# A modulation buffer of its own, loaded and applied by halves, and later modulation steps spread over four stages

## The chip, the cores and the metric

The kernel runs on one core of one Trainium2 chip. The metric is the device time of one execution in microseconds (us); lower is better. The engines that matter here are TensorE (PE, matrix products), VectorE (DVE), ScalarE (ACT), GpSimd (POOL) and the queues through which SyncE (SP), ACT and POOL issue their DMA transfers. Each engine runs its own list of instructions in a fixed order.

## The reference

The first of two transformer blocks is the one that the change touches; the second block behind it and the final norm are unchanged. Cut to what matters:

```
sh1, sc1, g1, sh2, sc2, g2 = split(silu(c) @ w_mod + b_mod, 6)          # latent rows; w_mod is 1024 x 6144
csh1, csc1, ...            = split(silu(c_ctx) @ w_mod + b_mod, 6)      # context rows
h_lat = rms_norm(x, norm_mix_g) * (1 + sc1) + sh1                       # 256 tokens x 1024
h_ctx = rms_norm(ctx, norm_mix_g) * (1 + csc1) + csh1                   # 256 tokens x 1024
p_lat, p_ctx = h_lat @ w_in, h_ctx @ w_in                               # 1024 x 9280: q, k, v, gates, ...
y_lat = token_mixer(...)      # gated delta rule (8 heads, chunks of 64, a triangular solve per chunk)
                              # + gated linear attention (4 heads), merged through gates
x = x + g1 * y_lat
h = rms_norm(x, norm_ffn_g) * (1 + sc2) + sh2
x = x + g2 * moe_ffn(h)       # top 4 of 32 experts, w_gu 32 x 1024 x 2048, w_down 32 x 1024 x 1024
```

Only `sh1, sc1, csh1, csc1` (columns 0 to 2047 of `w_mod`) are needed before the mixer. The columns 2048 to 6143 (`g1, sh2, sc2, g2`) are needed after it.

## The kernel before

**Head.** `pre` loads x and ctx over SP's queue, normalises them (ACT squares, DVE scales), and transposes the 512 tokens by 1024 features on PE into `xT` (L202, ACT copies L203). The modulation of the mixer is group 0 of `mod_steps`: eight steps k, and in each two tiles `w` of 128x1024 (512 KB) come over SP's queue (L161) into a ring of six buffers that all weight tiles share. Four matmuls a step (L162) add the product of the two conditioning vectors with the tile into one PSUM tile "mod". Behind the last step DVE adds the bias (L172), PE transposes (L178), DVE copies the result into `modT` (L180) and forms `sc1` (L209), DVE (L211) and ACT (L213) apply scale and shift to `xT`, and `split` makes the pair `hh` (high part, ACT, L49) and `hl` (low part, DVE, L50). Products in full precision are three matmuls of high and low parts (`mm3`, L76 to L78).

**Gates' weights and projections.** `gates` loads 64 columns of `w_in` into one more ring tile by two DMAs on ACT's queue (L259, L260: runs of 32 floats, 128 bytes), splits it into `whi`/`wlo` and makes the gates. `gdn_pair` works on two of the eight heads of the delta rule: six tiles of `w_in` (128x8x128, runs of 512 bytes) over POOL's queue (L399), q, k and v projections, a convolution on DVE (L372), and blocks of the triangular matrices that go through DRAM: stores `blkD` (L496) and loads `X` (L501), both on SP's queue. `L505` on DVE begins the triangular inverse of a pair: 31 pairs of DVE instructions (L515, L516), each of which needs the one before it. Its result goes out and back through SP's queue (L521 to L529), and PE's levels (L556 and on) and the scan follow. The four pairs overlap: the projections of pair n+1 stand ahead of the levels of pair n.

**Fill.** Behind each pair stand tasks that don't depend on the inverse, listed in `gdn`: `lat[0]` to `lat[15]` (`lat_act`: a projection of the latent rows, 48 matmuls, for the merge), and the 16 steps of `mod_steps(1)` and `mod_steps(2)`, whose tiles come over SP's queue (L161) into the same ring. Before:

```
fill = [lat[0:1] + m1[0:3] + lat[1:2] + m1[3:6] + lat[2:3] + m1[6:8],
        lat[3:4] + m2[0:3] + lat[4:5] + m2[3:6] + lat[5:6] + m2[6:8],
        lat[6:10], lat[10:] + [...]]
```

**What sets the order.** A scheduler puts each engine's instructions into one list when the program is built, from the order in which the code is written and from when buffers come free. On the chip each engine, and each DMA queue's issue, follows its list in order and waits where the next instruction's inputs or buffers aren't ready. Behind the mixer the 32 experts' weights are streamed (L1308, L1330), then block 2 follows.

Of the kernel before, what the change touches and what calls it, by code (L numbers as in the profile page):

```python
# [7 lines left out]
F32 = mybir.dt.float32  # L8
# [88 lines left out]
def pre(K, dbg=None):  # L97
# [8 lines left out]
    def G(shape=None):  # L106
        return psum.tile([P, 512], F32, name="g", bufs=2)
# [25 lines left out]
    nc.sync.dma_start(xc, I["ctx"].rearrange("o (t p) d -> p (o t) d", p=P))  # L133

# [14 lines left out]
    def mod_steps(g):  # L149


        hold = {}

        def step(k):
# [14 lines left out]
            for r in range(2 if g == 0 else 1):
                nc.gpsimd.dma_start(brow[r:P:32, :], bm)  # L170
            row = brow
            nc.vector.tensor_add(row, ps, brow)  # L172
            if g:
                nc.gpsimd.dma_start(K.modD[g - 1].rearrange("(q n) -> q n", n=512), row[0:P:32, :])
                return
            pt = G()
            for b in range(4):
                nc.tensor.transpose(pt[:, b * P:(b + 1) * P], row[:, b * P:(b + 1) * P], K.ident)  # L178
            for r in range(2):
                nc.vector.tensor_copy(K.modT[:, r].rearrange("p h (q b) -> p (h q) b", b=4),  # L180
                                      pt.rearrange("p (b q r) -> p r q b", b=4, r=32)[:, r])
# [17 lines left out]
    for k in range(8):  # L199
        p = G()  # L200
# [7 lines left out]
    for r in range(2):
        nc.vector.scalar_tensor_tensor(K.sc1[:, r], K.modT[:, r, 1], 1.0, K.nmg, op0=OP.add, op1=OP.mult)  # L209
    for k in range(8):  # L210
        nc.vector.tensor_scalar(xT[:, k, 0:256], xT[:, k, 0:256], K.sc1[:, 0, k:k + 1], K.modT[:, 0, 0, k:k + 1],  # L211
                                op0=OP.mult, op1=OP.add)
        nc.scalar.activation(xT[:, k, 256:512], xT[:, k, 256:512], AF.Identity, scale=K.sc1[:, 1, k:k + 1],  # L213
                             bias=K.modT[:, 1, 0, k:k + 1])
        split(K, xT[:, k, :], hh[:, k, :], hl[:, k, :])
# [15 lines left out]
def gates(K, dbg=None):  # L231
# [159 lines left out]
def gdn_pair(K, pr):  # L391
# [258 lines left out]
def gdn(K, dbg=None):  # L650
# [4 lines left out]
    m1, m2 = K.mod_steps(1), K.mod_steps(2)  # L655
    fill = [lat[0:1] + m1[0:3] + lat[1:2] + m1[3:6] + lat[2:3] + m1[6:8],
            lat[3:4] + m2[0:3] + lat[4:5] + m2[3:6] + lat[5:6] + m2[6:8],
            lat[6:10], lat[10:] + [lambda: gla_gates(K, 0), lambda: gla_proj(K, 0), lambda: gla_gates(K, 1)]]
# [1353 lines left out]
```

## Time and profile before

| | us |
|---|---|
| median of 3 runs | 2082.15 |
| fastest and slowest of them | 2078.74, 2091.74 |
| the profiled execution | 2083.65 |
| its span in the trace | 2081.9 |
| PE busy in the span | 1898.8 (91%) |
| DVE busy | 965.6 (46%) |
| ACT busy | 652.5 (31%) |

The mean granted TensorE clock was 0.954 of full speed. Times in the trace count from the start of the span. The head ends near 64 us, the four pairs of the delta rule reach to about 520 us, and from about 800 to 1700 us the experts' weights are streamed. Busy shares are means over stages that have different limits; what counts for a change in the first 500 us is who waits for whom there.

### The profile page before, as it was taken

How to read it: one execution, taken by the hardware profiler on the slowest of the kernel's cores; microseconds unless marked ns; L12 is line 12 of the kernel's file. 1: busy time of each engine (PE TensorE's matmuls, PEld its weight loads, DVE VectorE, ACT ScalarE, POOL GpSimd, SP SyncE). 2: the span in 40 equal slices, each digit the busy share in tenths (PEclk: the TensorE clock that was granted, in tenths of full speed). 3: DMA queues.
4: the chain of work that ended last, by engine and by line, in shares of the span. 5: the costliest groups of instructions: out<-in, count | busy, mean ns of one | idle time of the engine just before them, and what ended most of it. 6: DMA issues, size and time to landing. Idle time of an engine off the chain costs nothing. (4 is left out here: it accounts for less than half of the span.)

```text
span 2081.9 us, 27700 instructions
## 1 busy us (share of the span) xinstructions
PE 1898.8 (91%) x10742; PEld 1159.6 (56%) x10743; DVE 965.6 (46%) x2245; ACT 652.5 (31%) x1369; POOL 184.0 (9%) x247
## 2 busy tenths in 40 slices
PE   4796989799998999999999999999999889989998
PEld 1664768687986763333333333333333228779997
DVE  2797785857464641212122221221211137676777
ACT  2553545467554420000000000000000004555554
POOL 1343122211112000000000000000000000000000
PEclk8798999899999989999999999999999988998999
DMA  7347654437544689999999999999999994433551
GB/s 261 77 122 206 183 169 116 112 103 206 169 151 151 254 325 417 417 414 418 417 416 418 418 416 417 418 416 417 418 418 416 417 345 139 140 102 121 183 182 41
DMA packets 191939, 569.60 MB, mean 274 GB/s; under 512 B 47919, under 2 KB 90776, under 8 KB 158650
## 3 DMA queue, kind: packets, MB, share of 16 engines
q1 hardware_dynamic: 160064, 507.19, 63.1%
q0 software_dynamic: 13392, 47.72, 7.4%
q10 hardware_dynamic: 18346, 12.86, 2.5%
q8 instruction: 86, 1.41, 0.3%
q14 instruction: 51, 0.42, 0.1%
HBM read 555.22 MB, written 12.50 MB: 273 GB/s over the span
## 5 line engine op out<-in xcount | busy, mean ns | idle before, releaser
L50 DVE TENSOR_TENSOR wlo<-w,whi 128x1024 fp32r<-128x1024 f32 (+1 forms) x185 | 223.9, 1211 | 132.6 <-ACT whi L49 129.8
L1308 PE MATMUL pg<-w,xT 128*64 128x512 f32 x1024 | 274.4, 605 | 3.5 <-DMA w<-in_w_gu_dram 3.4
L1308 PE MATMUL pl<-w,xT 128*64 128x512 f32 x1024 | 268.1, 593 | 0.0
L49 ACT ACTIVATE whi<-w 128x1024 fp32r<-128x1024 f32 (+1 forms) x189 | 197.3, 1047 | 217.8 <-PE pj L77 70.4
L1330 PE MATMUL po<-w,aT 128*64 128x512 f32 x1024 | 239.9, 608 | 7.1 <-DMA w<-in_w_down_dram 5.7
L1230 ACT ACTIVATE th<-ga 128x512 f32<-128x512 f32 x32 | 20.2, 632 | 613.8 <-DVE ga L1228 613.8
L1338 DVE TENSOR_TENSOR o<-po,g 64x512 f32<-64x512 f32 x64 | 44.1, 689 | 260.1 <-PE po L1330 259.4
L1308 PEld LDWEIGHTS pl<-w,xT 128*64 128x64 f32 x1024 | 75.2, 137 | 146.4 <-issue 146.4
L1330 PEld LDWEIGHTS po<-w,aT 128*64 128x64 f32 x1024 | 69.5, 139 | 141.7 <-issue 121.9
L1308 PEld LDWEIGHTS pg<-w,xT 128*64 128x64 f32 x1024 | 65.2, 136 | 139.4 <-issue 115.9
L1228 DVE TENSOR_SCALAR ga<-pg 128x512 f32<-128x512 f32 x32 | 22.1, 691 | 244.8 <-PE pg L1308 244.8
L77 PE MATMUL pj<-wlo,hh 128*128 128x256 f32 x384 | 116.2, 303 | 2.8 <-DVE wlo L50 2.8
L76 PE MATMUL pj<-whi,hh 128*128 128x256 f32 x384 | 115.2, 300 | 2.9 <-ACT whi L49 2.9
L78 PE MATMUL pj<-whi,hl 128*128 128x256 f32 x384 | 114.6, 299 | 0.0
L76 PE MATMUL pj<-hh,whi 128*128 128x512 f32 (+1 forms) x264 | 100.9, 384 | 12.6 <-ACT hh L49 9.1
L372 DVE SCALAR_TENSOR_TENSOR acc<-padl,taps,acc 128x256 f32<-128x256 f32 x192 | 104.3, 557 | 10.1 <-ACT acc L365 8.0
L78 PE MATMUL pj<-hh,wlo 128*128 128x512 f32 (+1 forms) x264 | 100.0, 380 | 5.9 <-DVE wlo L50 5.7
L77 PE MATMUL pj<-hl,whi 128*128 128x512 f32 (+1 forms) x264 | 100.9, 382 | 0.1
L1288 POOL CAST se<-sel 128x128 fp32r<-128x128 f32 x32 | 22.4, 702 | 828.4 <-PE pl L1292 828.4
L1267 PEld LDWEIGHTS tr<-S,h 128*128 128x128 f32 x480 | 57.9, 191 | 48.6 <-issue 34.9
L77 PEld LDWEIGHTS pj<-wlo,hh 128*128 128x128 f32 x384 | 78.0, 203 | 11.0 <-DVE wlo L50 4.2
L1360 PE MATMUL y<-o,PwT 128*128 128x512 f32 (+1 forms) x136 | 72.2, 641 | 13.0 <-DVE o L1338 10.2
(682 smaller groups left out, 3601.7 us busy)
## 6 DMA issues: line engine op xcount, KB each, us to landing
w<-in_w_gu_dram SPq DMA_DIRECT2D x256, 1024.0 KB, 18.2
w<-in_w_down_dram SPq DMA_DIRECT2D x139, 1024.0 KB, 20.0
w<-in_w_in_dram POOLq DMA_DIRECT2D x72, 512.0 KB, 5.4
w<-in_w_mod_dram SPq DMA_DIRECT2D x48, 512.0 KB, 6.9
w<-in_w_up_dram SPq DMA_DIRECT2D x22, 1024.0 KB, 5.1
w<-in_w_in_dram SPq DMA_DIRECT2D x8, 1024.0 KB, 9.8
gbc<-gD ACTq DMA_DIRECT2D x16, 256.0 KB, 6.2
actD<-la ACTq DMA_DIRECT2D x16, 256.0 KB, 5.0
```

The lines of the kernel that those rows point to most:

```text
L49: K.nc.scalar.activation(hi, src, AF.Copy)
L50: (lo_eng or K.nc.vector).tensor_sub(lo, src, hi)
L76: nc.tensor.matmul(out, ah, bh, start=first, stop=False, **kw)
L77: nc.tensor.matmul(out, ah, bl, start=False, stop=False, **kw)
L78: nc.tensor.matmul(out, al, bh, start=False, stop=last, **kw)
L372: eng.scalar_tensor_tensor(al, pl[:, dy:dy + 4, dx:dx + 64], w, al, op0=OP.mult, op1=OP.add)
L1267: nc.tensor.matmul(p[:, kk * P:kk * P + m * CAP], h2[:, t, k * P:(k + 1) * P], S[:, t, e0:e1].rearrange("p e c -> p (e c)"), start=(kk == ...
L1288: nc.gpsimd.tensor_copy(se, sel[:, e, :, None].to_broadcast([P, 2, CAP]))
L1308: nc.tensor.matmul(pp[hs, :], xT[:, k, :], w[:, off + half * 512:off + half * 512 + 512], start=False, stop=(k == 7), skip_group_check=True)
L1330: nc.tensor.matmul(po[dh * CAP:(dh + 1) * CAP, :], aT[:, k % 4, (k // 4) * CAP:(k // 4 + 1) * CAP], w[:, kk * 1024 + dh * 512:kk * 1024 + ...
L1338: nc.vector.tensor_mul(outs[e // 2][e % 2 * CAP:(e % 2 + 1) * CAP, dh * 512:(dh + 1) * 512], po[hs], K.g2[hs])
L1360: nc.tensor.matmul(ps[dh], PwT[g][hs, t, :], outs[g][hs, dh * 512:(dh + 1) * 512], start=(g > 0), stop=True)
```

## The change

The head's modulation no longer goes through the ring. A buffer `wm` of its own holds all of group 0, loaded by 16 DMAs of 128x2x512 (512 KB each, runs of 2 KB); the first eight hold shift and scale for features 0 to 511, the second eight those for 512 to 1023. Between the halves comes the first `w_in` tile `w0`, behind them the gates' weights `wg`, and then the other five tiles of pair 0, all on SP's queue (before: ACT's and POOL's). The modulation is computed, transposed and applied one half after the other. In the fill, one modulation step stands behind each `lat` task, and the steps reach over three stages; the first three stages have four `lat` tasks each (before three, three and four).

```
+    w3 = I["w_in"].rearrange("o (k p) n -> p (o k) n", p=P)
+    K.wg = ring.tile([P, 8, P], F32, name="w")
+    nc.gpsimd.memset(K.wg[:, :, 64:], 0.0)
+    K.w0 = ring.tile([P, 8, P], F32, name="w")
+    wm = early.tile([P, 2, 8, 2, 512], F32, name="wm")
+    for b in range(2):
+        for k in range(8):
+            nc.sync.dma_start(wm[:, b, k], I["w_mod"][0, k * P:(k + 1) * P, 0:2048]
+                              .rearrange("p (s b n) -> p s b n", s=2, b=2)[:, :, b])
+        if b == 0:
+            nc.sync.dma_start(K.w0, w3[:, :, 0:P])
+        else:
+            nc.sync.dma_start(K.wg[:, :, 0:32], w3[:, :, 4096:4128])
+            nc.sync.dma_start(K.wg[:, :, 32:64], w3[:, :, 7200:7232])
...
-    for f in mod_steps(0):
-        f()
...
+    for b in range(2):
+        ps = psum.tile([P, 512], F32, name=("mod", "po")[b], bufs=1)
+        for k in range(8):
+            for s in range(2):
+                nc.tensor.matmul(ps[32 * s:32 * s + 32, :], csP[:, k, :], wm[:, b, k, s], start=(k == 0), stop=(k == 7),
+                                 skip_group_check=True)
+        nc.vector.tensor_add(rows[b], ps[:64], rows[b])
+        pt = G()
+        for i in range(4):
+            nc.tensor.transpose(pt[:, i * 64:(i + 1) * 64], rows[b][:, i * P:(i + 1) * P], K.ident[:64, :64])
...
+        for k in range(b * 4, b * 4 + 4):
+            nc.vector.tensor_scalar(xT[:, k, 0:256], xT[:, k, 0:256], K.sc1[:, 0, k:k + 1], K.modT[:, 0, 0, k:k + 1],
+                                    op0=OP.mult, op1=OP.add)
...
-    nc.scalar.dma_start(wg[:, :, 0:32], w3[:, :, 4096:4128])
-    nc.scalar.dma_start(wg[:, :, 32:64], w3[:, :, 7200:7232])
-    wgh, wgl = wsplit(K, wg, P)
+    wgh, wgl = wsplit(K, K.wg, P)
...
-    ws = []
-    for i in range(6):
+    ws = [] if pr else [K.w0]
+    for i in range(len(ws), 6):
         w = K.ring.tile([P, 8, P], F32, name="w")
         col = i % 3 * 1024 + pr * 256 + i // 3 * P
-        nc.gpsimd.dma_start(w, w3[:, :, col:col + P])
+        (nc.gpsimd if pr else nc.sync).dma_start(w, w3[:, :, col:col + P])
...
+    m = K.mod_steps(1) + K.mod_steps(2)
+    fill = [[f for i in range(4) for f in (lat[pr * 4 + i], m[pr * 5 + i])] + m[pr * 5 + 4:(pr + 1) * 5 + pr // 2]
+            for pr in range(3)]
+    fill.append(lat[12:] + [lambda: gla_gates(K, 0), lambda: gla_proj(K, 0), lambda: gla_gates(K, 1)])
```

Behind the edit at `pre` the line numbers are higher by 16 to 18: L161, L162, L172 of `mod_steps` become L176, L177, L187, the transposes of group 0 L227, `blkD` L513, `X` L518, L505 becomes L522, and L515/L516 become L532/L533.

**Place 1, SP's queue at the start of the program.** `w` are ring tiles, `gD` and `blkD` are DRAM tiles of the gates and of pair 0. Before:

```order
L132 DMA xlat<-in_x_dram 128x2x1024
L133 DMA xctx<-in_ctx_dram 128x2x1024
L161 DMA w<-in_w_mod_dram 128x1024 x16
L326 DMA gD<-grow 64x128
L161 DMA w<-in_w_mod_dram 128x1024 x4
```

SP's queue after:

```order
L132 DMA xlat<-in_x_dram 128x2x1024
L133 DMA xctx<-in_ctx_dram 128x2x1024
L142 DMA wm<-in_w_mod_dram 128x2x512 x8
L146 DMA w<-in_w_in_dram 128x8x128
L142 DMA wm<-in_w_mod_dram 128x2x512 x8
L148 DMA w<-in_w_in_dram 128x8x32
L149 DMA w<-in_w_in_dram 128x8x32
L416 DMA w<-in_w_in_dram 128x8x128 x5
L343 DMA gD<-grow 64x128
L176 DMA w<-in_w_mod_dram 128x1024 x2
```

The gates' weights and pair 0's tiles have moved onto this queue, behind the modulation's 16 transfers.

**Place 1, DVE at the end of the head.** `la` is the row of modulation values with its bias, `sc` is `sc1`. Before:

```order
L172 TENSOR_TENSOR la<-mod,la 128x512
L50 TENSOR_TENSOR wlo<-w,whi 128x1024
L180 COPY modT<-g 128x16 x2
L209 SCALAR_TENSOR_TENSOR sc_303<-modT,vecs 128x8
L50 TENSOR_TENSOR wlo<-w,whi 128x1024
L209 SCALAR_TENSOR_TENSOR sc_303<-modT,vecs 128x8
L211 TENSOR_SCALAR xT<-xT,sc_303,modT 128x256 x6
L50 TENSOR_TENSOR hl<-xT,hh 128x512 x2
L211 TENSOR_SCALAR xT<-xT,sc_303,modT 128x256 x2
L50 TENSOR_TENSOR hl<-xT,hh 128x512 x6
```

DVE there after:

```order
L224 TENSOR_TENSOR la<-mod,la 64x512
L230 COPY modT<-g 128x2x4 x2
L231 SCALAR_TENSOR_TENSOR sc_249<-modT,vecs 128x4 x2
L233 TENSOR_SCALAR xT<-xT,sc_249,modT 128x256 x4
L50 TENSOR_TENSOR hl<-xT,hh 128x512 x4
L224 TENSOR_TENSOR la<-po,la 64x512
L230 COPY modT<-g 128x2x4 x2
L231 SCALAR_TENSOR_TENSOR sc_249<-modT,vecs 128x4 x2
L233 TENSOR_SCALAR xT<-xT,sc_249,modT 128x256 x4
L50 TENSOR_TENSOR wlo<-w,whi 128x1024 x2
L50 TENSOR_TENSOR hl<-xT,hh 128x512 x4
```

The split of the gates' weights (`wlo`) stood between the bias and `modT`; it now stands behind both halves of the modulation, ahead of the last four `hl`.

**Place 2, PE at the first fill.** `pj_1391` is a projection of pair 1, `pj_1989` the one of `lat[0]`, `g_1436` a transpose of pair 1's keys, `w_2052` and on the modulation's tiles. Before:

```order
L78 MATMUL pj_1391<-hh_117,wlo_1388 128x512
L162 MATMUL mod_2051<-w_2060,csP_105 32x512
L162 MATMUL mod_2051<-w_2064,csP_105 32x512 x2
L162 MATMUL mod_2051<-w_2068,csP_105 32x512 x2
L162 MATMUL mod_2051<-w_2072,csP_105 32x512 x2
L162 MATMUL mod_2051<-w_2144,csP_105 32x512
L424 MATMUL g_1436<-ident_62,kT_1292 128x128 x4
L76 MATMUL pj_1989<-whi_1990,hh_117 128x256
```

PE there after (rows of `lat[0]` stand between `pj_1391` and the first of these):

```order
L78 MATMUL pj_1989<-whi_1990,hl_141 128x256
L76 MATMUL pj_1989<-whi_2018,hh_140 128x256
L177 MATMUL mod_2051<-w_2128,csP_128 32x512 x2
L177 MATMUL mod_2051<-w_2132,csP_128 32x512 x2
L76 MATMUL pj_2066<-whi_2067,hh_140 128x256
L441 MATMUL g_1436<-ident_62,kT_1292 128x128 x4
L177 MATMUL mod_2051<-w_2204,csP_128 32x512 x2
L77 MATMUL pj_1989<-wlo_2019,hh_140 128x256
```

The run of modulation matmuls behind `pj_1391` is gone; the first half of `lat[0]` stands in its place, and `g_1436` stands behind that.

**Place 2, DVE at the start of pair 0's inverse.** `acc` are the convolutions of pair 1, `L` and `X` the inverse of pair 0. Before:

```order
L372 SCALAR_TENSOR_TENSOR acc_1416<-padl1_346,taps_353,acc_1416 128x256
L459 TENSOR_TENSOR dk_1289<-d_1274,kds_464 128x8
L505 SCALAR_TENSOR_TENSOR L_991<-X_988,isd_470,L_991 128x1024
L372 SCALAR_TENSOR_TENSOR acc_1416<-padl1_346,taps_353,acc_1416 128x256
L507 MEMSET X_988 128x512
L378 SCALAR_TENSOR_TENSOR kT_1292<-th_1384,acc_1367 128x512
```

DVE there after:

```order
L476 TENSOR_TENSOR dk_1289<-d_1274,kds_466 128x8
L50 TENSOR_TENSOR wlo_1991<-w_1985,whi_1990 128x1024
L522 SCALAR_TENSOR_TENSOR L_991<-X_988,isd_472,L_991 128x1024
L524 MEMSET X_988 128x512
L389 SCALAR_TENSOR_TENSOR acc_1367<-padl0_348,taps_359,acc_1367 128x256
L526 MEMSET X_988 64x16 x2
L389 SCALAR_TENSOR_TENSOR acc_1367<-padl0_348,taps_359,acc_1367 128x256
L532 TENSOR_TENSOR xtmp_997<-L_991,X_988 128x31
```

The inverse begins ahead of twelve convolution taps that stood in front of it, and a split of `lat[0]`'s weights stands ahead of it.

**Place 3, SP's queue from pair 2's stores to pair 3's loads.** The rows between them that carry the inverse's result are left out. Before:

```order
L496 DMA blkD_2269<-mt 32x16x32 x4
L501 DMA X<-blkD_2269 64x1024 x2
...
L496 DMA blkD_3449<-mt 32x16x32 x4
L501 DMA X<-blkD_3449 64x1024 x2
```

SP's queue there after:

```order
L513 DMA blkD_2308<-mt 32x16x32 x4
L176 DMA w<-in_w_mod_dram 128x1024 x2
L518 DMA X<-blkD_2308 64x1024 x2
L176 DMA w<-in_w_mod_dram 128x1024 x4
...
L176 DMA w<-in_w_mod_dram 128x1024 x4
L513 DMA blkD_3532<-mt 32x16x32 x4
L176 DMA w<-in_w_mod_dram 128x1024 x2
L518 DMA X<-blkD_3532 64x1024 x2
L176 DMA w<-in_w_mod_dram 128x1024 x4
```

Sixteen loads of modulation tiles, each of which needs a free ring buffer, now stand among the transfers of pairs 2 and 3.

## Rows read from the trace of the kernel before

**Rows 1.** The page, section 4: the chain that ended last, by engine.

```profile
PE 16%; DVE 2%; ACT 1%; issue 0%; DMA 0%; DVEq 0%; ACTq 0%
```

**Rows 2.** DMA view, first 60 us: GB/s in 40 slices of 1.5 us.

```profile
GB/s 0 117 412 299 333 293 254 89 350 421 412 418 325 385 306 347 161 150 380 243 238 336 402 378 339 194 267 282 287 290 222 36 0 0 194 232 265 8 5 74
```

**Rows 3.** Waits in the first 60 us, SP's queue and PE: total, times, longest.

```profile
SPq L161 <- PE mod L162: 12.3, 5, 4.2
...
PE mod L162 <- DMA w<-in_w_mod_dram: 8.8, 5, 3.7
```

**Rows 4.** Timeline of the head: start, length, instruction, idle time before it.

```profile
6.56 23.70 SPq L161 DMA_DIRECT2D w<-in_w_mod_dram  x16
...
26.84 0.66 PE L202 MATMUL g<-ident,xn 128*128 128x128 f32 x4
...
30.66 1.10 ACTq L260 DMA_DIRECT2D w<-in_w_in_dram  x1
...
47.00 2.00 ACT L49 ACTIVATE whi<-w 128x1024 fp32r<-128x1024 f32 x2 [18.87 <-DMA w<-in_w_in_dram]
...
49.23 0.25 DVE L180 COPY modT<-g 128x16 f32<-128x16 f32 x2
...
51.90 1.14 ACT L49 ACTIVATE hh<-xT 128x512 fp32r<-128x512 f32 x2
...
52.57 1.01 PE L76 MATMUL pj<-hh,whi 128*128 128x512 f32 x2 [9.09 <-ACT hh L49]
...
64.63 0.38 PE L76 MATMUL pj<-hh,whi 128*128 128x256 f32 x1
```

**Rows 5.** Windows of the head: length, busy us of PE, PEld, DVE, ACT, POOL; PEclk, DMA share, GB/s.

```profile
12.00:20.00 8.00, 7.29 (x22) 1.49 (x22) 5.48 (x33) 1.23 (x3) 0.00 (x0) 1.00 0.99 387
...
40.00:46.00 6.00, 2.59 (x8) 0.71 (x4) 0.69 (x1) 0.00 (x0) 0.88 (x1) 0.50 1.03 284
```

**Rows 6.** DMA issues at 430 to 434.5 us: median us from issue to landing.

```profile
blkD<-mt SPq DMA_DIRECT2D x4, 64.0 KB, 2.8
```

**Rows 7.** Waits of PE at 60 to 200, 200 to 330 and 330 to 400 us.

```profile
PE mod L162 <- DMA w<-in_w_mod_dram: 17.9, 5, 8.3
...
PE mod L162 <- DMA w<-in_w_mod_dram: 11.1, 3, 5.8
...
PE pj L78 <- DVE wlo L50: 5.7, 1, 5.7
PE g L424 <- DVE kT L378: 3.9, 1, 3.9
```

**Rows 8.** Timeline of the first fill, PE and DVE.

```profile
165.53 1.91 PE L162 MATMUL mod<-w,csP 128*32 128x512 f32 x2 [8.31 <-DMA w<-in_w_mod_dram]
...
199.73 1.92 PE L162 MATMUL mod<-w,csP 128*32 128x512 f32 x4 [5.82 <-DMA w<-in_w_mod_dram]
...
162.64 1.28 DVE L505 SCALAR_TENSOR_TENSOR L<-X,isd,L 128x1024 f32<-128x1024 f32 x1
...
201.75 0.69 DVE L172 TENSOR_TENSOR w<-mod,w 128x512 f32<-128x512 f32 x1 [6.77 <-PE mod L162]
...
218.45 0.48 DVE L372 SCALAR_TENSOR_TENSOR acc<-padl,taps,acc 128x256 f32<-128x256 f32 x1
...
220.93 0.17 DVE L516 TENSOR_TENSOR X<-X,xtmp 128x16 f32<-128x16 f32 x1
```

**Rows 9.** Windows of the first fill and of the experts' stream, columns as in rows 5.

```profile
150.00:200.00 50.00, 32.06 (x187) 19.62 (x188) 40.33 (x128) 22.46 (x57) 12.82 (x16) 0.84 0.75 205
...
900.00:1300.00 400.00, 383.69 (x1726) 139.91 (x1728) 81.41 (x136) 27.62 (x48) 9.85 (x13) 1.00 1.02 416
```

**Rows 10.** Pair 3's load and inverse (timeline), and SP's longest wait at 60 to 500 us for a modulation tile.

```profile
434.98 1.11 SPq L501 DMA_DIRECT2D X<-blkD  x2
...
447.96 1.27 DVE L505 SCALAR_TENSOR_TENSOR L<-X,isd,L 128x1024 f32<-128x1024 f32 x1
...
SPq L161 <- POOL wlo L50: 42.6, 1, 42.6
```

More of the change, by code (lines that the diff above doesn't have):

```diff
@@ L165, in step @@
                 return
-            brow = K.ring.tile([P, 512], F32, name="w") if g else K.wsp.tile([P, 512], F32, name="la", bufs=2)
+            brow = K.ring.tile([P, 512], F32, name="w")
             nc.gpsimd.memset(brow, 0.0)
             bm = I["b_mod"][0, g * 2048:(g + 1) * 2048].rearrange("(q n) -> q n", n=512)
[L169 to L181, printed above, removed]
+            nc.gpsimd.dma_start(brow[0:P:32, :], bm)
+            nc.vector.tensor_add(brow, ps, brow)
+            nc.gpsimd.dma_start(K.modD[g - 1].rearrange("(q n) -> q n", n=512), brow[0:P:32, :])
         return [lambda k=k: step(k) for k in range(8)]
@@ L203, in pre @@
         nc.scalar.activation(xT[:, k, :], p, AF.Copy)
-    for f in mod_steps(0):
-        f()
     K.sc1 = c.tile([P, 2, 8], F32, name="sc1")
[L208 to L215, printed above, removed]
+    rows = []
+    for b in range(2):
+        row = K.wsp.tile([64, 512], F32, name="la", bufs=2)
+        nc.gpsimd.memset(row, 0.0)
+        for r in range(2):
+            nc.gpsimd.dma_start(row[r:64:32, :], I["b_mod"][0, 0:2048].rearrange("(s b n) -> s b n", s=2, b=2)[:, b])
+        rows.append(row)
+    for b in range(2):
+        ps = psum.tile([P, 512], F32, name=("mod", "po")[b], bufs=1)
[7 more added lines that the diff above has]
+            nc.tensor.transpose(pt[:, i * 64:(i + 1) * 64], rows[b][:, i * P:(i + 1) * P], K.ident[:64, :64])
+        bs = slice(b * 4, b * 4 + 4)
+        for r in range(2):
+            nc.vector.tensor_copy(K.modT[:, r, :, bs], pt[:, :256].rearrange("p (i s r) -> p r s i", s=2, r=32)[:, r])
+            nc.vector.scalar_tensor_tensor(K.sc1[:, r, bs], K.modT[:, r, 1, bs], 1.0, K.nmg[:, bs], op0=OP.add, op1=OP.mult)
+        for k in range(b * 4, b * 4 + 4):
+            nc.vector.tensor_scalar(xT[:, k, 0:256], xT[:, k, 0:256], K.sc1[:, 0, k:k + 1], K.modT[:, 0, 0, k:k + 1],
+                                    op0=OP.mult, op1=OP.add)
+            nc.scalar.activation(xT[:, k, 256:512], xT[:, k, 256:512], AF.Identity, scale=K.sc1[:, 1, k:k + 1],
+                                 bias=K.modT[:, 1, 0, k:k + 1])
+            split(K, xT[:, k, :], hh[:, k, :], hl[:, k, :])
     if dbg and "hT" in dbg:
@@ L255, in gates @@
     nc.vector.tensor_copy(K.taps, pc[:, :216])
-    wg = K.ring.tile([P, 8, P], F32, name="w")
-    nc.vector.memset(wg[:, :, 64:], 0.0)
-    w3 = I["w_in"].rearrange("o (k p) n -> p (o k) n", p=P)
-    nc.scalar.dma_start(wg[:, :, 0:32], w3[:, :, 4096:4128])
-    nc.scalar.dma_start(wg[:, :, 32:64], w3[:, :, 7200:7232])
-    wgh, wgl = wsplit(K, wg, P)
+    wgh, wgl = wsplit(K, K.wg, P)
     ps = psum.tile([P, 512], F32, name="pj", bufs=2)
@@ L654, in gdn @@
     lat = [lambda i=i, cg=cg: lat_act(K, i, cg) for i in range(4) for cg in range(4)]
[L655 to L658, printed above, removed]
+    m = K.mod_steps(1) + K.mod_steps(2)
+    fill = [[f for i in range(4) for f in (lat[pr * 4 + i], m[pr * 5 + i])] + m[pr * 5 + 4:(pr + 1) * 5 + pr // 2]
+            for pr in range(3)]
+    fill.append(lat[12:] + [lambda: gla_gates(K, 0), lambda: gla_proj(K, 0), lambda: gla_gates(K, 1)])
     g = gdn_pair(K, 0)
```

## Prediction, made before the changed kernel ran

> **What bounds the kernel now.** I read the chain of waits first [rows 1]. It gives single lines at most a few per cent and PE 16% as a whole, so it names no single owner: the answer has to come from the stages. The stage behind the mixer is settled quickly. In the experts' stream the 16 DMA engines are booked at a share of 1.02 and PE is busy for 383.7 of 400 us [rows 9], so nothing that starts there can shorten it, and a microsecond saved ahead of it starts the whole stream a microsecond earlier. I count what is gained or lost in the first 500 us at 1:1.
>
> In the head the order of reading is the queue, then the wait, then the engine. SP waits 12.3 us in five pieces for PE to free ring buffers, PE 8.8 us for the tiles [rows 3], and the throughput shows holes at those places: slices of 89, 161 and 150 GB/s between slices of 412 to 421 [rows 2]. The 16 modulation tiles are issued over 23.7 us [rows 4]. The gates' weights, issued by 30.7 us, end ACT's idle time of 18.9 us only at 47.0 [rows 4]; `modT`, whose transposes need none of them, is copied at 49.23, because DVE has the gates' split ahead of it; PE begins the gates' projection at 52.57 after 9.1 us of waiting for `hh` [rows 4]. So the head is bound by when bytes arrive and by an order that lets the last of them hold all the rest.
>
> In the fills PE waits for modulation tiles: 17.9 us in five waits at 60 to 200 us and 11.1 us in three behind that [rows 7]. But PE is not alone there. In the first fill DVE is busy 40.3 of 50 us and PE 32.1 [rows 9], and pair 0's inverse, begun at 162.64, ends at 221.1, with one stop of 6.8 us inside it for a modulation result [rows 8].
>
> **The change part by part.** The sum is made against the profiled execution, 2083.65 us, which is 1.5 above the median of 2082.15.
>
> *Head, transfers.* By 12 us the first eight slices of 1.5 us have moved 2.70 MB [rows 2] (their sum is 1797 GB/s, by 1.5). Up to the end of half 1 there are x, ctx, 16 times 0.524 MB and `w0`, 11.01 MB, so 8.31 are left: 7.79 MB in 2-KB runs and 0.52 in 512-byte runs. No 2-KB run is in the rows; bounds are 284 GB/s, where 512-byte runs alone fill the engines, and 387, where 4-KB runs do [rows 5]. With a fixed cost for each run through these two points, 2-KB runs come at 368, an estimate. 7.79/0.368 + 0.52/0.284 = 23.0 us: half 1 has landed at 35.0 (34.0 at 387, 41.3 at 284). The gates' weights follow alone, 2048 runs of 128 bytes. The nearest rows are four stores of 512 such runs each, 2.8 us to landing [rows 6], with the load that reads them issued 4.2 us behind the first; their 0.26 MB at 368 would take 0.7. I take 4.2, as the runs are alike: 39.2, between 34.7 (34.0 + 0.7) and 45.5 (41.3 + 4.2).
>
> A rule of the Trainium skill speaks against this place for them: page "DMA: Bandwidth & Descriptors", section "Specifications", gives 512 bytes as the smallest transfer that reaches line rate, with a read-modify-write below it. The store rows agree in kind (0.26 MB in up to 4.2 us is 62 GB/s); no row shows such a load alone. By line rate the head would be 3.5 us better than I count, and a price of several times the stores' would take the gain away; both lie inside the ends kept below.
>
> *Head, compute.* Half 0 is there near 22 us and its matmuls run between the transposes, which end at 27.5 [rows 4]; its scale, shift and split for features 0 to 511 lie under the loads and cost nothing while the loads last. Half 1 is summed at about 36 and its `modT` no longer stands behind the gates' split. From the landing of the gates' weights on, ACT does two splits of 1.0 us (2.00 for both), then for four k's a scale (about 0.55) and an `hh` (about 0.57) [rows 4] (1.14 for two), and DVE the last `hl`: some 7.8 us, so hh and hl are whole at 47.0. PE starts its first gate matmul at about 41.3 (split high, split low) where it started at 52.57. It needs 64.63 - 52.57 = 12.1 us from there to the next projection, with which it fills the wait for the late k's: 41.3 + 12.1 = 53.4 at the latest, perhaps a microsecond less, as the first twelve matmuls need not wait for `hh`. That is 11.2 to 12 us earlier. **I take -12**; with the gates' weights at 34.7 it would be -16, at 45.5 -6, and at 47.0, where they land now, still about -4, since `hh` for half the features is ready.
>
> What hides the loads that were moved: pair 0's other five tiles come behind the gates' weights on the same queue; at 284 GB/s they need 9.2 us, the first is there at about 41, and PE uses them from 53 on. The last one waits for the gates' ring buffer, free when the split has read it, at 42; it is used last. Cost zero.
>
> *First fill.* The modulation matmuls behind `pj_1391` go (place 2), and with them PE's waits of 8.3 and 5.8 us and DVE's stop of 6.8 [rows 8]. I don't count them as a gain. DVE needs 40.3 us of every 50 here, and what stood in front of the inverse, twelve convolution taps of 0.48 us [rows 8], 5.8 us, is moved into it. `g_1436`, which PE runs behind part of `lat[0]`, needs keys whose taps are among these. So PE waits for DVE in the place of the DMA, and a split of `lat[0]`'s weights, which ACT must begin, stands ahead of the inverse. The inverse gets shorter by the stop that goes (6.8) and longer by the taps (5.8); PE has up to 15 us of `lat[0]` and less modulation done at that point. These don't add up to a sign: **0, between -10 and +6**.
>
> *Second fill.* 11.1 us of waits [rows 7] stand behind a clump of tiles; spread out behind `lat` tasks, most have a task to hide them. DVE takes part of it, as above: **-4, between 0 and -11**.
>
> *Third fill.* The stages of pairs 2 and 3 have more `lat` work ahead of the last fill (12 tasks for 10). At 330 to 400 us PE now waits 5.7 us for a split and 3.9 for keys [rows 7], beside an inverse on DVE: filler for about half of it, **-5, between 0 and -9**.
>
> *Last fill.* Five modulation steps stand in the third fill, and their last tiles come in a clump whose matmuls stand together. The like clump now costs 11.1 in three waits: **+4, between 0 and +11**.
>
> *Small parts.* The head keeps its 32 modulation matmuls (two for each of 16 steps in the place of four for each of 8) and gets four transposes, an add and a few small copies more, half of them under the loads: 0. POOL's queue loses the six loads of pair 0 and gets two of the bias: 0, as nothing waits for POOL's issue there.
>
> Sum: -12 + 0 - 4 - 5 + 4 = **-17**: 2083.65 - 17 = 2066.6, and against the median 2065.
>
> **The rivals.** *All waits go.* PE's waits for modulation tiles, 17.9 + 11.1, pass to the end in full and DVE keeps up: -12 - 25 with a few left, 2045 to 2050. For it: DVE's own stop of 6.8 us vanishes as well. Against it: DVE at 40 of 50 us. *The head alone, or less.* The fills give nothing, 2083.65 - 12 - 1.5 = 2070; or the gates' weights land as late as now, and 2078 is left. For it: twelve taps moved into the chain of pair 0, and small runs last. *Slower.* SP's queue runs in order, and two modulation tiles stand ahead of `X` of pair 2, four ahead of pair 3's `blkD`, two more ahead of its `X` (place 3). Now nothing stands there, and a modulation tile on that queue waits up to 42.6 us for a ring buffer [rows 10]. The inverse of pair 3 begins 13.0 us behind the issue of its load [rows 10]; that is the slack. If the buffers come free later than that at both pairs, each of which could lose 42.6 - 13.0 = 29.6 us, the time is 2065 + 30 to 2065 + 59: 2095 to 2124. For it: the row; against it: pair 0 has had such tiles ahead of its load already, and there the buffers come free from splits that run ahead. *It doesn't do what it says.* The halves overlap nothing, because the first projections stand behind both; then the gain is the ring's 12.3 us of queue waits less what the small runs cost, 2072 or so, inside the second rival.
>
> **How the numbers follow.** A difference under about 1%, 21 us, is what a measurement of this kernel can hardly tell from none; faster by that means below 2061.3. My own case, 50%, reaches from 2056 to 2073 and is below 2061.3 for two fifths of its chance, 0.20. All waits go: 0.18. Head alone or less: 0.25. Slower: 0.07, all of it beyond 1%. That makes faster 0.38, same 0.55, slower 0.07. The range for 8 in 10 leaves out the slower case and the outer part of the first rival: 2047 to 2079.
>
> **What would show it.** Right: no wait of SP for "mod" in the first 35 us and 350 to 380 GB/s without holes up to there; ACT's gate split ends its wait at 38 to 41; the first gate matmul at 40 to 43 and the next projection near 53; in the first fill waits of PE for DVE (kT, whi, wlo) in the place of those for modulation tiles; pair 0's inverse from about 150 to 200. Wrong: a wait of ACT for the gates' weights beyond 45; PE without new waits in the first fill, which would be the first rival; an `X` load of pair 2 or 3 that SP issues late behind a modulation tile, with DVE idle behind it, which would be the slower one. The sum would also be wrong if the shift in the first 500 us were not found again at the start of the experts' stream.

## The result, and the profile after

The changed kernel takes 2096.07 us (median of 14 runs, 2091.59 to 2102.85), the one before 2085.94 beside it (14 runs, 2076.31 to 2092.97). The ratio is 1.0057 [1.0040, 1.0075], with its 95% interval: 10 us slower by the medians, 12 by the ratio, where 17 us faster was forecast. The profiled execution took 2099.48 us with a span of 2097.8.

First the head. The DMA view of the changed kernel, first 60 us, in slices of 1.5 us; then its windows of the head (columns as in rows 5); then its waits there; then its timeline.

```profile
GB/s 0 85 404 390 409 164 198 315 395 392 381 389 386 367 316 360 385 392 385 385 388 382 246 75 285 221 335 289 238 95 301 237 153 0 0 0 210 139 0 164
```

```profile
12.00:20.00 8.00, 6.85 (x15) 1.43 (x16) 5.51 (x33) 1.27 (x4) 0.00 (x0) 1.00 1.05 389
28.00:34.00 6.00, 4.71 (x25) 1.40 (x24) 2.50 (x9) 2.56 (x6) 0.00 (x0) 1.00 1.08 366
```

```profile
SPq L416 <- DVE wlo L50: 4.5, 1, 4.5
...
PE mod L222 <- DMA wm<-in_w_mod_dram: 4.4, 1, 4.4
```

```profile
6.59 6.94 SPq L142 DMA_DIRECT2D wm<-in_w_mod_dram  x8
...
16.01 9.16 SPq L142 DMA_DIRECT2D wm<-in_w_mod_dram  x8
...
27.13 4.48 SPq L149 DMA_DIRECT2D w<-in_w_in_dram  x1
...
30.68 0.68 DVE L224 TENSOR_TENSOR la<-mod,la 64x512 f32<-64x512 f32 x1 [13.10 <-PE mod L222]
...
31.82 7.06 PE L222 MATMUL po<-wm,csP 128*32 128x512 f32 x32
...
36.52 1.99 ACT L49 ACTIVATE whi<-w 128x1024 fp32r<-128x1024 f32 x2
...
38.99 0.68 DVE L224 TENSOR_TENSOR la<-po,la 64x512 f32<-64x512 f32 x1 [1.56 <-issue]
...
40.13 0.50 PE L76 MATMUL pj<-hh,whi 128*128 128x512 f32 x1
```

The two holes of 161 and 150 GB/s at 24 to 27 us [rows 2] are gone: behind 10.5 us no slice up to 33 us is under 315. A hole of 164 and 198 GB/s stays at 7.5 to 10.5 us. SP's waits up to there are for small loads, as before, and the slice of 89 [rows 2] was no wait for the ring, though the prediction reads it so: in the kernel before, SP has no wait for "mod" in the first 12.5 us. SP's wait for "mod" of 12.3 us [rows 3] is gone too. ACT splits the gates' weights at 36.52 instead of 47.00, and PE starts the gates' projection at 40.13 instead of 52.57 [rows 4]. The head did what it was to do.

The milestones show where the lead goes. Each is a time of the profiled execution less that of the kernel before (whose own times stand in the first row), in us; minus is earlier. "Inverse" is the first instruction of a pair's triangular inverse; the pairs count from 0 to 3. Each column rests on one execution of each kernel: the five kernels with the old head, whose order is the same there, begin the first projection at 46.8 to 54.0 us, so a difference of some 7 us in this table can be chance.

| kernel | ratio [95%] | first projection | inverse 0 | inverse 1 | inverse 2 | inverse 3 | first expert matmul |
|---|---|---|---|---|---|---|---|
| before, its times | 1 | 52.6 | 162.6 | 251.3 | 349.5 | 448.0 | 759.9 |
| after | 1.0057 [1.0040, 1.0075] | -12.4 | -11.2 | -13.1 | +5.6 | +19.3 | +19.5 |
| head changed, old fills (e1) | 1.0003 [0.9986, 1.0021] | -12.0 | -8.4 | -14.2 | +2.0 | +0.8 | +1.3 |
| e1 with a later head (e11) | 1.0123 [1.0101, 1.0144] | +1.4 | +4.6 | +0.6 | +21.0 | +21.8 | +24.9 |
| old head, new fills (e2) | 1.0075 [1.0047, 1.0103] | -2.4 | +0.1 | -7.4 | +0.3 | +13.2 | +19.1 |
| head in one piece, old fills (e12) | 0.9955 [0.9938, 0.9972] | -12.2 | -9.4 | -9.0 | -3.0 | -6.7 | -3.4 |
| head in one piece, new fills (e14) | 1.0035 [1.0017, 1.0054] | -12.1 | -11.7 | -20.7 | -12.3 | +0.3 | +8.6 |

In the changed kernel 18.7 us are lost between the inverses of pairs 1 and 2, and 13.7 between those of pairs 2 and 3. The first loss comes with the changed head (e1 16.2, e11 20.4), the second with the new lists (e2 13.0, e14 12.6). What PE waits for in these 500 us, before and then after (the view of waits, 60 to 560 us: total, times, longest):

```profile
PE mod L162 <- DMA w<-in_w_mod_dram: 23.3, 7, 8.3
PE g L424 <- DVE kT L378: 10.2, 4, 3.9
...
PE pj L78 <- DVE wlo L50: 5.7, 1, 5.7
PE sc L556 <- DMA AB<-solD: 5.0, 4, 3.5
...
PE pj L76 <- ACT whi L49: 2.9, 2, 1.7
PE pj L77 <- DVE wlo L50: 2.8, 3, 1.7
```

```profile
PE g L441 <- DVE kT L395: 15.8, 5, 5.7
PE pj L78 <- DVE wlo L50: 15.4, 3, 11.9
PE sc L573 <- DMA AB<-solD: 10.2, 3, 6.9
PE mod L177 <- DMA w<-in_w_mod_dram: 10.1, 4, 3.4
PE pj L76 <- ACT whi L49: 6.0, 3, 4.3
PE pj L77 <- DVE wlo L50: 5.0, 5, 1.6
```

The wait for modulation tiles went from 23.3 to 10.1, as meant. In its place came waits for the halves of the split of the other weights (`wlo`, `whi`), for keys (`kT`) and for the inverse's result (`AB`): 26.6 us in five rows before and 52.4 after. The windows from the start to the first expert's matmul, and from the end of pair 2's inverse to the start of pair 3's, before and then after; behind them the first of these windows in e2:

```profile
0.00:759.90 759.90, 653.34 (x4554) 526.68 (x4555) 505.90 (x1353) 390.33 (x900) 158.29 (x211) 0.91 0.56 170
...
395.50:448.00 52.50, 49.65 (x508) 46.24 (x509) 28.33 (x75) 31.03 (x72) 11.59 (x16) 0.84 0.51 122
```

```profile
0.00:779.50 779.50, 668.37 (x4560) 535.52 (x4561) 511.00 (x1357) 388.46 (x898) 154.60 (x209) 0.90 0.53 165
...
398.70:467.20 68.50, 66.87 (x652) 58.55 (x651) 45.08 (x121) 44.45 (x113) 16.17 (x20) 1.00 0.50 133
```

```profile
0.00:779.00 779.00, 655.10 (x4556) 533.20 (x4557) 504.28 (x1353) 385.72 (x896) 161.07 (x211) 0.90 0.54 165
```

Two things are to be seen. First, PE has the same work in both (4554 and 4560 matmuls) and is busy 15.0 us longer: of the 19.5 us, most is not idle time but the same matmuls taking longer. In e2 the 19.1 us are idle time, 123.9 for 106.6, and PE is busy 1.8 us longer. So a like loss shows as slower matmuls in the one profile and as idle time in the other; that it is one and the same is not shown. Second, work has been pushed from the inverses, where DVE sets the pace, into the gap before pair 3's inverse, which PE fills: 652 matmuls for 508, and 68.5 us for 52.5.

### The profile page after: what moved, and what is told of

It reads as the page before. It is cut to its first block, busy times and chain, and to the rows that moved or that the text cites. A ratio compares the mean times of both kernels' runs of the same rounds, so it can differ in the third digit from the quotient of the medians.

```text
span 2097.8 us, 27698 instructions
## 1 busy us (share of the span) xinstructions
PE 1909.6 (91%) x10746; PEld 1165.0 (56%) x10747; DVE 970.6 (46%) x2249; ACT 650.8 (31%) x1367; POOL 180.2 (9%) x245
## 5 line engine op out<-in xcount | busy, mean ns | idle before, releaser
L76 PEld LDWEIGHTS pj<-whi,hh 128*128 128x128 f32 x384 | 77.2, 201 | 18.0 <-ACT whi L49 9.7
## 6 DMA issues: line engine op xcount, KB each, us to landing
w<-in_w_in_dram SPq DMA_DIRECT2D x8, 1024.0 KB, 19.3
```

What stands on the lines that cost most here:

```text
L76: nc.tensor.matmul(out, ah, bh, start=first, stop=False, **kw)
```

## The experiments

Every kernel was timed in five rounds beside the kernel before. e5 and e11 add small transfers and leave nothing out.

**e1, the head alone.** The changed head, and `fill` as before.

```
-    m = K.mod_steps(1) + K.mod_steps(2)
-    fill = [[f for i in range(4) for f in (lat[pr * 4 + i], m[pr * 5 + i])] + ...
+    fill = [lat[0:1] + m1[0:3] + lat[1:2] + m1[3:6] + lat[2:3] + m1[6:8], ...    # as before
```

> The changed head (own buffer, halves, gates' weights last, pair 0's tiles on SP's queue) with the fill lists of the kernel before. Theory P (the head gains 12 to 14 us, as the changed kernel's trace shows 13.8 at the start of pair 0's inverse, and the new fill lists lose some 25): 10 to 14 us faster than before, 0.993 to 0.995. Rival R (the head's lead is spent in the first fills whatever the lists, since VectorE sets the pace there): within 4 us of before. Rival S (the moved loads of the head themselves disturb pair 1): slower than before.

Measured: 1.0003 [0.9986, 1.0021]: theory P's number is refuted, and rival R's came. (The 13.8 us that the expectation reads at pair 0's inverse are 11.2 in the table.) The lead is 14.2 us at the start of pair 1's inverse and gone at the start of pair 2's.

**e2, the fills alone.** The head of before, and `fill` of after.

> The head of the kernel before with the new fill lists. Theory P: 20 to 28 us slower than before, 1.010 to 1.013, and the head's lead missing at the start of pair 0's inverse. Rival R: 8 to 14 us slower, as the changed kernel was, since the head's lead counts for nothing. Rival S: within 4 us of before.

Measured: 1.0075 [1.0047, 1.0103], so the fills cost some 16 us by themselves, between theory R's and theory P's price. Pair 0's inverse did end earlier, 205.3 for 221.1, but the gap before pair 3's inverse grew to 66.9 us.

**e3, e4, the two halves of the new lists**, each in the changed kernel. e3 keeps the spread steps and takes the old counts of `lat` (3, 3, 4, 6); e4 keeps four `lat` a stage and takes the old clumps of modulation steps.

```
e3: fill = [lat[0:1] + m[0:1] + lat[1:2] + m[1:2] + lat[2:3] + m[2:5], lat[3:4] + m[5:6] + lat[4:5] + m[6:7] + lat[5:6] + m[7:10], ...
e4: fill = [lat[0:1] + m1[0:3] + lat[1:2] + m1[3:6] + lat[2:3] + m1[6:8] + lat[3:4], ...
```

> The changed kernel, but the gates' projection tasks stand as before (three, three, four and six in the four fills) and only the modulation steps are spread, five, five and six to a fill, one behind each task. Theory P1 (the two tasks that were moved ahead of the last inverse are the loss: they stood beside it as cover, and now stand where TensorE has no gap): 8 to 14 us faster than before. Rival Q (the spread modulation steps are the loss, by their loads on SP's queue and in the ring): as slow as the changed kernel, 1.004 to 1.008.

> The changed kernel, but the modulation steps stand in the first two fills in groups of three, three and two as before, and only the projection tasks are four to a fill. Theory P1 (task counts are the loss): as slow as the changed kernel, 1.004 to 1.010. Rival Q (the spread modulation steps are the loss): 8 to 14 us faster than before.

Measured: 1.0064 [1.0040, 1.0088] and 1.0089 [1.0062, 1.0115]. Neither half gives the loss back, so neither theory holds for both runs.

**e5, e11, the same order with a later head.** e1, with one (e11) or two (e5) round trips of 4 KB ahead of the gates' split, so that nearly the same order of instructions starts later.

```
+    hop = K.dram.tile([P, 8], F32, name="hop")
+    for _ in range(2):                              # e11: range(1)
+        nc.gpsimd.dma_start(hop, K.wg[:, :, 63])
+        nc.gpsimd.dma_start(K.wg[:, :, 63], hop)
```

> The changed head with the fill lists of before, and four small transfers in a chain put between the landing of the gates' weights and their split, so that the head ends some 8 to 12 us later (its trace says by how much) while the order on the engines stays the same but for about ten rows. If the head is on the path in this order (V: the 12 us were lost because the scheduler wrote another order behind the head): as much slower as the delay, 1.004 to 1.006. If the lead was spent because the stages behind have slack for it (W): within 4 us of the same kernel without the delay, 0.999 to 1.002.

> The head-alone kernel with one pair of small transfers in a chain between the landing of the gates' weights and their split, so that its head ends within some 6 us of where that of before does; the order is that of the head-alone run but for some ten rows. Theory V (that order costs 12 to 14 us at an equal head): 1.005 to 1.008. Rival W: 0.999 to 1.002.

Measured: e11 1.0123 [1.0101, 1.0144], e5 1.0132 [1.0110, 1.0154]. Both are slower than either theory had it. Against e1, e11 is 13.4 us later at the first projection and 23.5 at the first expert; e5 is 26.5 later there and 33.2 at the first expert (794.4 for 761.3). A delay of the head is not swallowed: it comes out at least whole. And e11, whose first projection is only 1.4 us later than that of the kernel before, is 1.2% slower than it. So e1 did not lose its lead because the head doesn't bound the end; it runs behind the head in a worse order. That order costs some 13 us in e1, about what the lead gives, and more in e11 (+1.4 us at the first projection, +24.9 at the first expert). The loss has one place: between the inverses of pairs 1 and 2 e1, e11 and e5 lose 16.2, 20.4 and 21.0 us, and the kernels with a new head and the old order behind it (e9, e12) 9.3 and 6.0.

**e6, e7, e8, other lists with the old head.** e6 has two `lat` in each of the first two stages, e7 one more in the second, e8 the old counts with the steps spread as in e3.

```
e6: fill = [lat[0:1] + m1[0:4] + lat[1:2] + m1[4:8], lat[2:3] + m2[0:4] + lat[3:4] + m2[4:8], lat[4:10], ...
e7: second stage + lat[6:7], third stage lat[7:10]
e8: 5, 5 and 6 modulation steps in stages 1 to 3, lat 3, 3, 4
```

> The kernel before with two projection tasks in each of the first two fills (before three, changed kernel four), modulation steps eight and eight as before. Theory T (tasks that stand ahead of a pair's weights in the ring delay that pair's projections and so its inverse, and leave less work to cover the last one): 4 to 12 us faster than before. Rival U (these tasks are the cover of the second and third inverse, and any shift of the balance costs): 4 to 15 us slower.

> The kernel before with one projection task more in the second fill (three, four), nothing else moved. Theory T: 5 to 9 us slower, half of what two tasks cost, and the last inverse starts 5 to 9 us later. Rival U: also slower, but by waits beside the inverses, with the last inverse on time.

> The kernel before, with only the modulation steps spread (five, five, six, one behind each projection task of the first three fills), the tasks' counts three, three, four, six as before. Theory T alone (only the counts matter): within 4 us of before. Rival Q (the spread of the steps costs by itself, since the last six steps now come behind the last pair's weights, where the trace of the like kernel with the new head lost 8 us between the last scan and the experts): 8 to 14 us slower.

Measured: 1.0119 [1.0093, 1.0146], 1.0077 [1.0053, 1.0101], 1.0115 [1.0094, 1.0137]. Fewer tasks ahead, more tasks ahead and only spread steps are all slower, by more than either theory had it. No count of tasks alone explains that.

**e9, e10, the gates' weights between the halves.** e1 and the changed kernel, each with `wg` loaded ahead of half 1.

```
         if b == 0:
+            nc.sync.dma_start(K.wg[:, :, 0:32], w3[:, :, 4096:4128])
+            nc.sync.dma_start(K.wg[:, :, 32:64], w3[:, :, 7200:7232])
             nc.sync.dma_start(K.w0, w3[:, :, 0:P])
```

> The changed head and the fill lists of before, as in the head-alone run, but the gates' weights are loaded between the two halves of the modulation and not last. The scheduler then writes behind the head the order of the kernel before (it differs from it in head rows alone). Theory V (the head's lead passes 1:1, and the head-alone run lost it to the other order that the late gates' weights brought about): 10 to 16 us faster than before, 0.992 to 0.995. Rival W (the lead is spent behind the head in any order): within 4 us of before.

> The changed kernel with the gates' weights loaded between the two halves and not last; behind the head its order is that of the run with the old head and the new fill lists, which was 1.0075. Theory V: that less the head's 12 us, 0.999 to 1.003. Rival W: 1.006 to 1.009, as slow as that run.

Measured: e9 0.9990 [0.9974, 1.0005], e10 1.0058 [1.0038, 1.0077]. Theory V is missed in both; e9's number is rival W's, e10's next to it. In e9 only the head's rows differ from the order of before. Its head gains less, as these rows of its timeline show (PE, then ACT):

```profile
34.51 0.61 PE L76 MATMUL pj<-hh,whi 128*128 128x512 f32 x2 [1.72 <-ACT hh L49]
...
50.37 1.09 ACT L234 ACTIVATE xT<-xT,modT,sc 128x256 f32<-128x256 f32 x2 [13.37 <-DVE sc L230]
```

The projections begin at 34.51, but stand ahead of half 1's modulation on PE, and ACT waits 13.37 us for it. The lead is 4.7 us at pair 0's inverse, in the slowest of its twelve executions; in the time some 2 are left, with no difference inside the interval.

**e12, e13, the buffer without the halves.** `wm` in one piece in runs of 4 KB, modulation, `modT` and `sc1` as before, pair 0's tiles behind it on SP's queue, old fills. The gates' weights come behind the first 8 of the 16 transfers (e12) or behind all (e13).

```
+    wm = early.tile([P, 8, 2048], F32, name="wm")
+    for k in range(8):
+        for s in range(2):
+            nc.sync.dma_start(wm[:, k, s * 1024:(s + 1) * 1024], I["w_mod"][0, k * P:(k + 1) * P, s * 1024:(s + 1) * 1024])
+        if k == 3:                                  # e13: k == 7
+            nc.sync.dma_start(K.wg[:, :, 0:32], w3[:, :, 4096:4128])
+            nc.sync.dma_start(K.wg[:, :, 32:64], w3[:, :, 7200:7232])
```

> The modulation's own buffer alone: all 16 tiles of group 0 loaded without waiting for the ring (runs of 4 KB), the gates' weights behind the first eight and pair 0's tiles behind all of it on SP's queue, but the modulation is computed and applied in one piece as before, and the fills are those of before. Behind the head the order is that of before. The last modulation matmul should come near 35 us for 41.5, and the first projection near 40 for 52.6, a lead of 11 to 13 us. Theory V (a lead passes 1:1 where the order behind is that of before): 9 to 13 us faster than before, 0.9935 to 0.9955. Rival W (a lead is spent behind the head in any order, only delays pass): within 4 us of before.

> The kernel with the modulation's own buffer, in one piece, and the fills of before (0.9955), with one difference: the gates' weights are loaded behind all 16 modulation tiles in the place of behind eight. The order changes in some 80 rows around pairs 0 and 1 on TensorE. If the late weights cost by themselves, by the order and by holding the gates' projection: 0.998 to 1.003. If they cost only together with the halves: 0.994 to 0.997.

Measured: e12 0.9955 [0.9938, 0.9972], 2074.57 us; e13 0.9962 [0.9946, 0.9979], 2076.67. Of the 4554 instructions that PE runs up to the first expert some 80 stand elsewhere in e12 than in before, all but two of them in the first 66 us, and its lead of 12 us at the first projection is 9.4 us in the time, as theory V had it. It beats both kernels. It starts the projection as early as the changed kernel does:

```profile
40.35 0.62 PE L76 MATMUL pj<-hh,whi 128*128 128x512 f32 x2 [2.25 <-ACT hh L49]
```

So the halves bring nothing beyond the buffer that these runs can tell, and with the buffer in one piece the gates' weights cost nothing by standing last.

**e14, e15, other fills on the better head.** e14 is e12 with the fills of after. e15 is e12 with 5 steps in the first stage, 11 in the second and none in the third.

```
e15: fill = [lat[0:1] + m[0:1] + lat[1:2] + m[1:2] + lat[2:3] + m[2:5],
             lat[3:4] + m[5:9] + lat[4:5] + m[9:13] + lat[5:6] + m[13:16], lat[6:10], ...
```

> The kernel with the modulation's own buffer, in one piece, and the changed kernel's fill lists; behind the head its order is that of the run with the old head and the new lists (1.0075). Theory V (head and lists add up): 1.001 to 1.005. Rival (the lists suit an earlier head better): 0.995 to 0.999.

> The kernel with the modulation's own buffer, in one piece; tasks three, three, four, six as before, but only five modulation steps in the first fill and the other eleven in the second, none behind the last pair's weights. Theory S (what costs in the spread lists is the steps that pass to the third fill): within 4 us of the kernel with the lists of before, 0.993 to 0.998. Rival (any shift of steps between the fills costs): 1.002 to 1.008.

Measured: e14 1.0035 [1.0017, 1.0054], which is 0.8% over e12, as e2 is over before (0.9955 times 1.0075 is 1.0030): head and lists add up. e15 1.0110 [1.0085, 1.0136], with a gap of 69.3 us before pair 3's inverse: that steps in the third stage are the cost is refuted, as it has none there.

## Why the prediction was wrong

**The head: the number was right, its path in part by luck.** -12 was taken; -12.4 was found at the first projection and -11.2 at pair 0's inverse. (Five traces with the old head begin the projection at 50.9 us on average, four with the changed one at 39.8.) By themselves the 2-KB runs moved at 389 GB/s, as fast as 4-KB runs (387 [rows 5]), for the 368 estimated. The gates' weights moved between 32.8 and 35.9 us, 3.1 us for the 4.2 taken, and ACT split them from 36.52 without a wait, ahead of the 38 to 41 forecast. Half 1 was summed at 38.99 for 36, since its matmuls kept PE until 38.88. So the first gate matmul, forecast at 41.3 behind the gates' split, came at 40.13 behind half 1: two misses that cancel. The 128-byte runs set nothing at the end: e13, with them behind everything, and e12 stand at 0.9962 and 0.9955, inside their intervals. The Trainium skill (page "DMA: Bandwidth & Descriptors", section "Specifications") gives 512 bytes as the smallest transfer that reaches line rate. The trace agrees in kind: 0.26 MB in 3.1 us, beside some 2-KB runs.

**"I count what is gained or lost in the first 500 us at 1:1": the step that failed first.** It holds for the way from the first expert's matmul on (+19.5 there, +15.9 in the span), and nearly for a head with the old order behind it (e12: 12 us become 9.4). It doesn't hold for this head: its -12 became 0 (e1), because the halves together with the gates' weights last made the scheduler write another order behind the head. Up to the first expert some 320 of PE's 4554 instructions and 150 of DVE's 1353 stand elsewhere in e1 than in before (in e12 some 80 and 7, nearly all in the head), far outside the three places that the prediction looked at. How it lost the lead is seen at pair 3's projections, whose tiles POOL's queue loads in order. POOL, ACT and PE in e1's timeline, then POOL's load in that of before:

```profile
309.85 2.69 POOL L416 DMA_DIRECT2D w<-in_w_in_dram  x3 [4.85 <-PE mod L177]
...
313.52 0.28 PE L78 MATMUL pj<-whi,hl 128*128 128x256 f32 x1
...
319.69 1.06 ACT L49 ACTIVATE whi<-w 128x1024 fp32r<-128x1024 f32 x1 [10.83 <-DMA w<-in_w_in_dram]
...
320.80 0.58 PE L76 MATMUL pj<-hh,whi 128*128 128x256 f32 x1 [7.00 <-ACT whi L49]
...
325.76 1.70 PE L573 MATMUL sc<-AB,mt 32*32 32x32 f32 x32 [4.17 <-DMA AB<-solD]
...
327.98 0.41 PE L77 MATMUL pj<-hl,whi 128*128 128x256 f32 x1
```

```profile
301.56 0.93 POOL L399 DMA_DIRECT2D w<-in_w_in_dram  x1
```

The load stands behind a modulation step whose matmuls end late, 8.3 us later than in before although pair 1's inverse began 14.2 us earlier; the weights are split at 319.69, and PE stands still for 7.00 us and then 4.17. The windows of these 15 us, e1 and then before (PE's busy time is the second number):

```profile
310.00:315.00 5.00, 3.80 (x31) 2.80 (x23) 0.69 (x1) 0.00 (x0) 4.93 (x6) 1.00 0.82 118
315.00:320.00 5.00, 0.00 (x0) 0.00 (x0) 0.00 (x0) 0.31 (x1) 0.00 (x0) 0.57 1.05 287
320.00:325.00 5.00, 0.80 (x2) 0.50 (x2) 3.44 (x4) 2.34 (x4) 2.71 (x3) 0.50 1.15 263
```

```profile
310.00:315.00 5.00, 1.53 (x18) 1.37 (x18) 3.61 (x10) 3.68 (x12) 3.84 (x5) 1.00 0.96 237
315.00:320.00 5.00, 5.00 (x42) 4.94 (x40) 1.90 (x7) 1.38 (x5) 0.00 (x0) 0.66 1.11 293
320.00:325.00 5.00, 4.74 (x64) 4.52 (x63) 2.88 (x4) 2.18 (x4) 1.06 (x2) 1.00 0.85 106
```

PE is busy 4.6 us here for 11.3. Milestones on PE agree: e1 is 13.0 us ahead of before at pair 2's keys (276.0 for 289.0), 7.6 ahead at the first levels of pair 1 (307.2 for 314.8), and 3.0 behind at the next (325.8 for 322.8). The part ahead of these stops goes in two waits for modulation tiles, 4.7 and 4.4 us at 278 to 291 us, where before has one of 4.2. That e1's order and not its early start costs the lead is shown by e11, which has e1's order behind the head; that these waits are the place where it goes is read from the trace and was not tried by itself.

**First fill, 0 between -10 and +6.** In the changed kernel pair 0's inverse ran from 151.46 to 204.64 (150 to 200 forecast), 5.3 us shorter than before, inside the ends; in e2 it is 15.9 shorter, outside them.

**Second fill -4, third -5, last +4: -5 in sum, and its sign failed.** e2 and e14 put the lists at +16 us, with either head. The third fill is the term that failed most: from the start of pair 2's inverse to that of pair 3's, where -5 was taken, the four traces with the new lists (after, e2, e10, e14) lose 12.6 to 13.7 us against before, and the six others with the old ones (e1, e5, e9, e11, e12, e13) between -3.8 and +0.8. The term took two more `lat` tasks as filler beside an inverse. It left out that all weights go through the six ring buffers in the order of the lists, so that a task that is put earlier puts its tiles ahead of pair 3's weights. POOL's queue after, where it loads these (before: 301.56 to 313.95); then a group of PE's matmuls between the end of pair 2's inverse and the start of pair 3's, after:

```profile
325.08 1.81 POOL L416 DMA_DIRECT2D w<-in_w_in_dram  x2 [1.02 <-DMA modD<-w]
...
347.73 1.76 POOL L416 DMA_DIRECT2D w<-in_w_in_dram  x2 [20.84 <-PE mod L177]
...
358.54 1.76 POOL L416 DMA_DIRECT2D w<-in_w_in_dram  x2 [9.05 <-PE sc L647]
```

```profile
L76 PE MATMUL pj<-hh,whi 128*128 128x512 f32 (+1 forms) x25 | 9.1, 363 | 0.0
```

POOL waits 20.84 us for a buffer that a modulation step holds. The last of pair 3's tiles is loaded 4 us behind the start of pair 2's inverse, in the traces with the old lists 29 to 42 us ahead of it. So with the new lists 71 to 77 of pair 3's 144 projection matmuls (three groups like the one above) stand in the gap between the two inverses, with the old ones none, and the gap lasts 66.9 to 68.5 us for 47.9 to 52.5. The "filler for half of it" pushed needed work into the gap: beside the four inverses PE runs 1104 matmuls before, 1007 after and 875 in e2. I counted the waits that go, and named the wait that would come for DVE, but gave it a price only inside the first fill. It is in the rows: for modulation tiles 13.2 us fewer, for `wlo`, `whi`, `kT` and `AB` 25.8 more.

**What of the lists costs is settled in part.** Spread steps (e8), four tasks a stage (e4), fewer (e6), one more (e7) and two stages only (e15) are each 0.8 to 1.6% slower than the lists of before on the same head. Where pair 3's projections come late the gap is long: some 19 of their matmuls stand in it with spread steps (e3, e8; 57.5 and 56.3 us), 64 with four tasks a stage (e4; 64.5 us), 45 with two stages only (e15; 69.3 us). In e6 and e7 there are none or one, the gap is 42.9 and 51.4 us, and 18 and 10 us are lost behind pair 3's inverse, which stays open. No run moved pair 3's loads alone, so that they are the cause is read from the traces and not tried; nor was a larger ring.

**The rivals.** The slower one gave the sign and not the mechanism. SP's queue after, around pair 3's loads:

```profile
447.33 2.53 SPq L513 DMA_DIRECT2D blkD<-mt  x4
...
454.86 0.83 SPq L176 DMA_DIRECT2D w<-in_w_mod_dram  x2
455.87 1.14 SPq L518 DMA_DIRECT2D X<-blkD  x2
```

Two modulation tiles do stand ahead of `X`, but `X` is issued 6.0 us behind the end of the stores, for 29.6 us priced; the stores themselves came late (430 to 434.5 in the kernel before [rows 6]), and they waited for DVE's `mt`, 8.1 us, and not for a tile. With the load as close behind the stores as in before, some 4 of the 19 us would be saved. The tiles that held up pair 3 stood in the ring, ahead of its weights. "All waits go" is refuted by the waits. "The head alone" is refuted by e2, as the lists cost 16 us; its price for the head holds nearly in e12 (9.4 us) and not in e1 (0). "It doesn't do what it says" is refuted by the timeline, as half 0 is summed at 30.68 and half 1 at 38.99, though e12 shows that nothing came of it. One slip of the chances: of 2056 to 2073, spread evenly, three tenths and not two fifths lie below 2061.3; no conclusion hangs on it.

## What to carry to other kernels

Where a scheduler writes the order, a local edit of the head may reorder stages that the diff doesn't touch; compare the whole order first, and test the edit once in a form that leaves the order behind it alone (here the buffer in one piece: 9.4 us, where the halves with the gates' weights last gave 0). Work that goes through a shared ring has a price in everything that passes through the ring behind it: before a filler task is moved ahead, name the tiles that it delays and the step that waits for them. A wait that is taken from one engine is counted as gained only where the next-latest producer of the same consumer has been read from the trace.

## What was unexpected in the hardware

A stop of PE cost more than its length, as the work behind it ran at a lower granted clock. In e1's windows above PE stands still from 313.8 to 320.8 us, and the granted clock is 0.57 and then 0.50, the lower of its two levels (1.2 of 2.4 GHz); a matmul of 128x256 that took 0.28 us ahead of the stop takes 0.41 behind it. At 150 to 400 us the clock is 0.82 after and 0.90 before, and the same matmuls up to the first expert take 668.4 us of PE for 653.3. How much of this the clock makes is not shown: in e2 the clock is 0.84 in that stretch, and PE is busy only 1.8 us longer than before.

A round trip of 4 KB through DRAM ahead of the gates' split cost 13 us, and not because the queues were full: the first projection stands at 40.6 in e1, 54.0 in e11 and 67.0 in e5, where the DMA engines are booked at a share of 0.10 from 51 to 66 us. POOL's waits for the first store, the first load back and the second store in e5, and ACT's wait for the whole:

```profile
51.99 0.93 POOL L281 DMA_DIRECT2D w<-hop  x1 [12.81 <-DMA hop<-w]
55.27 0.85 POOL L280 DMA_DIRECT2D hop<-w  x1 [2.36 <-DMA w<-hop]
62.88 0.90 POOL L281 DMA_DIRECT2D w<-hop  x1 [6.75 <-DMA hop<-w]
...
65.93 2.00 ACT L49 ACTIVATE whi<-w 128x1024 fp32r<-128x1024 f32 x2 [20.96 <-DMA w<-hop]
```
